# Storing the RWKV states from GpSimd's queue, with the prompt state in another buffer

## The chip, the core and the metric

The kernel runs on one core of one Trainium2 chip. The core has a matrix engine (TensorE, PE in the profile, with its weight loads shown apart as PEld), three engines for elementwise work (VectorE or DVE, ScalarE or ACT, GpSimd or POOL) and a queue engine (SyncE or SP) that does nothing here but issue DMAs. Each engine takes its instructions in a fixed order. The metric is the time of one execution on the device in microseconds; lower is better.

## The reference

One step of a streaming encoder with one layer, for a prompt of 256 tokens and 8 sample sequences of 16 tokens, 384 tokens in all, with a model width of 1024. Cut to what matters here:

```
P = h @ w_in                                  # RWKV part, attention part, two gates
# RWKV-7, 16 heads of 64; for every token, in order:
sa = einsum('bhij,bhj->bhi', S, a)
S  = S * w + sa[..., None] * b + v[..., None] * k
y  = einsum('bhij,bhj->bhi', S, r)
...
m = gate_a * (o_a @ w_proj_a) + gate_b * (o_b @ w_proj_b)
x = x + g1 * (m @ w_out)
x = x + g2 * peer(rmsnorm(x) ...)             # 16,384 experts, top-k
```

The final state `S` of every sequence is an output: `wkv_prompt` (16 heads of 64 x 64) and `wkv_sample` (8 times as much). Nothing else in the program reads these outputs.

## The kernel before, in words

The program has four stages: the input and its modulation; a long stage with RWKV, attention, gates and the rest of the modulation; the mix of both branches; and the experts, which take more than half of the time. The change is in the second stage.

There the method `run` goes through a string `ORDER` and emits one unit of work for each letter: R is a pair of RWKV heads (eight of them, numbered 0 to 7 by `e`), D a quarter of the attention heads, G a gate unit, M a modulation unit. The written program is a list; a planner then makes the order of each engine's queue from it, by simulated time, taking the earlier-written instruction first when several are ready. So on the chip the units overlap, and a later unit fills what an earlier one leaves free. The planner also adds every wait that a buffer or a value needs. When the program changes, all orders are made anew.

Buffers go by tag. In the RWKV pool a tag has one buffer, if not said otherwise, and tiles with one tag take turns in the order in which they are written in the program: a tile can be filled only when all that reads or writes the tile before it, stores included, is done.

One RWKV pair (`rwkv_pair`) goes so:

- Front: three projections `r`, `k`, `v`, elementwise work, and the matrices `MB`, `MK`. The gate's weights are loaded into the tag `gup` (L559, L560) and serve only at the pair's end.
- `rwkv_inverse`: a triangular inverse. Its 16 x 16 blocks are solved row by row on VectorE (L708, L710) between several DMA round trips through DRAM (L693 to L722). Then two levels merge the blocks. Each level begins with a GpSimd multiplication into the tag `NO` (L727), which PE reads at once (`cp<-TN,NO` in the profile), and ends with L742.
- `chain_p`: the prompt's four chunks in sequence. The states `H` are written from L791 on, the last one at L805, and L806 stores it.
- `chain_s`: the eight samples. Their states are loaded (L828) into the tag `S0`, updated (L875), multiplied by a decay on GpSimd (L877) and stored (L878).
- End: normalisation and the gate; L686 stores the pair's output to DRAM, and the mix loads the outputs of all pairs at L1185.

The pairs overlap: the front, the row-by-row solution and the first `NO` of pair e+1 are made while pair e is in its chains. The two levels of pair e+1 use a PSUM tag (`cp`) that both chains use too.

The lines on which the prediction's steps rest:

```python
726:  NO = self.t([128, 4, 64], tag="NO")
727:  nc.gpsimd.tensor_tensor(NO, MB[:, :, 0:64], ..., op=OP.mult)
770:  H = self.t([128, 4, 64], tag="gup")
806:  nc.sync.dma_start(self.O["wkv_p"][:, e], H[:, 3])
877:  nc.gpsimd.tensor_tensor(S0, S0, ..., op=OP.mult)
878:  nc.sync.dma_start(self.O["wkv_s"][:, e], S0)
```

Weights come through SP: `raw` (L248) loads 512 KB at a time into the tag `w`, which has four buffers; ScalarE and VectorE split them (L238, L242) for PE, while the modulation units read them as they are.

Of the kernel before, what the change touches and what calls it, by code (L numbers as in the profile page):

```python
# [19 lines left out]
OP = mybir.AluOpType  # L20
# [163 lines left out]
S0, PH = 30, 4  # L184
# [17 lines left out]
class K:  # L202
# [342 lines left out]
    def rwkv_pair(self, e):  # L545
# [106 lines left out]

        H = lambda t: t.rearrange("p i (h d) -> p i h d", d=64)
        B = lambda s: s.unsqueeze(3).to_broadcast([128, 3, 2, 64])
        sm = self.t([128, 3, 2], tag="gnm")
        nc.vector.tensor_reduce(out=sm, in_=H(y), op=OP.add, axis=AX.X)
        nc.vector.tensor_scalar(sm, sm, 1.0 / 64, None, op0=OP.mult)
        nc.vector.tensor_tensor(H(y), H(y), B(sm), op=OP.subtract)
        sq = self.t([128, 3, 128], tag="sq2")
        nc.scalar.activation(sq, y, AF.Square)  # L660
        vr = self.t([128, 3, 2], tag="gnv")
        nc.vector.tensor_reduce(out=vr, in_=H(sq), op=OP.add, axis=AX.X)
        rs = self.rstd(vr, vr, 1.0 / 64, GN_EPS)
        nc.vector.tensor_tensor(H(y), H(y), B(rs), op=OP.mult)
        lw = self.t([128, 2, 128], tag="lnx")
# [3 lines left out]
        L = lambda q: lw[:, q].unsqueeze(1).to_broadcast([128, 3, 128])  # L669
        nc.gpsimd.tensor_tensor(H(vn), H(vn), B(bon), op=OP.mult)  # L670
        nc.gpsimd.tensor_tensor(vn, vn, L(1), op=OP.add)
# [73 lines left out]
    def chain_p(self, e, AR, M, TT, bn, kn, vn, y, DC):  # L745

        nc = self.nc
        MB, MK = M  # L750
        hs = lambda h: slice(h * 64, h * 64 + 64)
        units = [(i, c, h, slice(64 * c, 64 * c + 64), slice(64 * h, 64 * h + 64)) for i in range(2) for h in range(2) for c in range(2)]
        Sb = self.t([128, 3, 2, 64], tag="Sb")
        nc.gpsimd.memset(Sb, 0.0)

        p = self.ps([128, 2, 2, 128], tag="cp")
        for i in range(2):
            nc.tensor.transpose(p[:, i, :, 0:64], AR[:, 0, 2 * i:2 * i + 2].rearrange("p a b -> p (a b)"), self.ident)
        for i, c, h, rr, hr in units:
            self.mm(p[rr, i, h, 64:128], MK[rr, i, h, 0:64], vn[rr, 1 + i, hs(h)], tp=(64 * c, 64 * c))  # L760
        R = self.t([128, 2, 2, 128], tag="S0")
        nc.scalar.activation(R, p, AF.Copy)

        p = self.ps([128, 2, 2, 128], tag="cp")
        for i, c, h, rr, hr in units:
            self.mm(p[rr, i, h], TT[rr, i * 2 + h], R[rr, i, h], tp=(64 * c, 64 * c))
        Q = self.t([128, 2, 2, 128], tag="cQ")
        nc.vector.tensor_copy(Q, p)

        H = self.t([128, 4, 64], tag="gup")  # L770
        G = self.t([128, 3, 64], tag="NX")
        Y = self.t([128, 3, 64], tag="lnx")
        for c, tag in ((0, "cp"), (1, "cs")):
            p = self.ps([128, 3, 2, 64], tag=tag)
            rr = slice(64 * c, 64 * c + 64)
            for i in range(2):
                hh = [(h, slice(64 * h, 64 * h + 64), (64 * c, 64 * h)) for h in range(2)]
                for h, hr, to in hh:
                    self.mm(p[hr, 0, i], bn[rr, 1 + i, hs(h)], Q[rr, i, h, 64:128], start=True, stop=False, tp=to)
                for h, hr, to in hh:  # L780
                    self.mm(p[hr, 0, i], kn[rr, 1 + i, hs(h)], vn[rr, 1 + i, hs(h)], start=False, stop=True, tp=to)
                if i or c:
                    for h, hr, to in hh:
                        self.mm(p[hr, 1, i], Q[rr, i, h, 0:64], bn[rr, 1 + i, hs(h)], tp=to)
                    for h, hr, to in hh:
                        self.mm(p[hr, 2, i], Q[rr, i, h, 0:64], MB[rr, i, h, 64:128], tp=to)
            un = slice(c, 4, 2)
            i0 = 0 if c else 1
            ug = slice(c + 2 * i0, 4, 2)
            u1 = slice(c + 2 * i0 - 1, 3, 2)  # L790
            nc.vector.tensor_tensor(H[:, un], p[:, 0], DC[:, un].unsqueeze(2).to_broadcast([128, 2, 64]), op=OP.mult)  # L791
            nc.vector.tensor_tensor(G[:, u1], p[:, 1, i0:], self.i64.unsqueeze(1).to_broadcast([128, 2 - i0, 64]), op=OP.add)
            nc.vector.tensor_tensor(Y[:, u1], p[:, 2, i0:], AR[:, 1, ug], op=OP.add)
        for h in range(2):
            hr = slice(64 * h, 64 * h + 64)
            nc.vector.tensor_copy(Sb[hr, 0, h], H[hr, 0])
        for un in range(1, 4):
            p = self.ps([128, 64], tag="cp")
            for h in range(2):
                hr = slice(64 * h, 64 * h + 64)  # L800
                self.mm(p[hr], G[hr, un - 1], Sb[hr, un - 1, h], tp=(64 * h, 64 * h))
            for h in range(2):
                hr = slice(64 * h, 64 * h + 64)
                out = Sb[hr, un, h] if un < 3 else H[hr, 3]
                nc.vector.scalar_tensor_tensor(out, p[hr], DC[hr, un:un + 1], H[hr, un], op0=OP.mult, op1=OP.add)  # L805
        nc.sync.dma_start(self.O["wkv_p"][:, e], H[:, 3])  # L806
        p = self.ps([128, 2, 128], tag="cp")
        cc = [(c, slice(64 * c, 64 * c + 64)) for c in range(2)]
        for i in range(2):
            for c, rr in cc:  # L810
                un = 2 * i + c
                if un:
                    self.mm(p[rr, i], Y[:, un - 1], Sb[:, un - 1].rearrange("p a b -> p (a b)"), start=(un == (2, 1)[c]), stop=False, tp=(0, 64 * c))
        for i in range(2):
            for h in range(2):
                for c, rr in cc:
                    self.mm(p[rr, i, hs(h)], MB[rr, i, h, 64:128], Q[rr, i, h, 64:128], start=False, stop=False,
                            tp=(64 * c, 64 * c))
                for c, rr in cc:
                    self.mm(p[rr, i, hs(h)], MK[rr, i, h, 64:128], vn[rr, 1 + i, hs(h)], start=False, stop=True,  # L820
                            tp=(64 * c, 64 * c))
        self.cpr = nc.scalar.activation(y[:, 1:3], p, AF.Copy)

    def chain_s(self, e, AR, M, TT, bn, kn, vn, y, DC):
        nc = self.nc
        MB, MK = M
        S0 = self.t([128, 8, 64], tag="S0")
# [36 lines left out]
        for g0 in (0, 2):  # L864
            pp = [self.ps([128, 128], tag=tag) for tag in ("cs", "cp")]
            for q, (src, x) in enumerate(zip((bi, ki), ex)):
                for h in range(2):
                    for gp, p in zip((g0, g0 + 1), pp):
                        gr = slice(32 * gp, 32 * gp + 32)
                        m = self.mm(p[64 * h:64 * h + 64], src[gr, hs(h)], x[gr, h].rearrange("p j d -> p (j d)"), start=(q == 0),  # L870
                                    stop=(q == 1), tp=(32 * gp, 64 * h))
                        if gp == g0 and q == 0:
                            self.after(m, self.cpr)
            for gp, p in zip((g0, g0 + 1), pp):
                self.cpr = nc.vector.tensor_tensor(S0[:, 2 * gp:2 * gp + 2], S0[:, 2 * gp:2 * gp + 2],  # L875
                                                   p.rearrange("p (j d) -> p j d", d=64), op=OP.add)
        nc.gpsimd.tensor_tensor(S0, S0, DC.unsqueeze(2).to_broadcast([128, 8, 64]), op=OP.mult)  # L877
        nc.sync.dma_start(self.O["wkv_s"][:, e], S0)  # L878


    def rope(self, dst, x, which, n):
# [914 lines left out]
```

## Time and profile before

| | |
|---|---|
| median of three runs | 1747.88 us (1744.3 to 1750.02) |
| the profiled execution's own time | 1744.26 us |
| its span, first to last instruction | 1742.5 us |
| PE busy | 1666.7 us (96%) |
| VectorE busy | 1353.8 us (78%) |
| ScalarE busy | 745.2 us (43%) |
| GpSimd busy | 544.0 us (31%) |
| DMA, mean | 251 GB/s |

The span is what the profile covers; the execution's own time has 1.8 us more. PE's ends are modelled, so its busy time is not time at its peak; its idle time is what the waits are read from. The state stores are 8 x 256 KB (`out_wkv_s`) and 8 x 32 KB (`out_wkv_p`), the first at 257.2 us, the last at 683.3 us.

### The profile page before, as it was taken

The page shows a single profiled execution, that of the slowest core. Times are in us where ns is not written, and L with a number is a line of the kernel's source. Part 1 is how long each engine was busy: PE and PEld are TensorE (multiplying, and loading weights), DVE is VectorE, ACT ScalarE, POOL GpSimd, SP SyncE. Part 2 cuts the span into 40 slices and gives each one's busy share as a digit, 9 for nine tenths or more (in the row PEclk, how much of TensorE's full clock was granted, in tenths as well). Part 3 has the DMA queues.
Part 4 walks back from the last instruction along what each step waited for, and adds up shares of the span by engine and source line. Part 5 has one row for each costly group of instructions (what it writes and reads, how often), then busy time and mean ns, then how long its engine had stood idle before and what let it go on. Part 6 is the DMA issues. An engine that isn't in the chain of part 4 may idle for free.

```text
span 1742.5 us, 33102 instructions
## 1 busy us (share of the span) xinstructions
PE 1666.7 (96%) x12376; PEld 1407.1 (81%) x12376; DVE 1353.8 (78%) x2905; ACT 745.2 (43%) x1666; POOL 544.0 (31%) x621
## 2 busy tenths in 40 slices
PE   6999999999999988999999999999989999999997
PEld 4998888877888877998887889999966676776675
DVE  3548878776877865566999998999948788777797
ACT  4543433333343333444323355577844343443343
POOL 2434333232333220034033233441233234332331
PEclk8999999899999999999999999999999999999999
DMA  8543653455365365755398999986479999999993
GB/s 300 167 135 104 209 181 85 135 176 165 91 208 158 97 220 193 250 186 193 122 359 318 368 345 383 392 317 236 165 286 351 368 384 372 395 385 382 353 395 109
DMA packets 173049, 437.23 MB, mean 251 GB/s; under 512 B 46036, under 2 KB 86612, under 8 KB 156504
## 3 DMA queue, kind: packets, MB, share of 16 engines
q1 hardware_dynamic: 154456, 300.89, 50.8%
q0 software_dynamic: 18432, 134.23, 19.8%
q8 instruction: 98, 1.61, 0.4%
q14 instruction: 63, 0.52, 0.1%
HBM read 403.75 MB, written 31.30 MB: 250 GB/s over the span
## 4 chain that ended last, share of the span: by engine, by line
PE 42%; DVE 16%; DMA 6%; issue 5%; ACT 3%; POOL 1%; SPq 0%; DVEq 0%; POOLq 0%; ACTq 0%
PE mm L234 11%; PE fx L234 10%; PE dx L234 8%; PE cp L234 6%; PE bx L234 5%; DVE acc L1616 2%; DVE wl L242 2%; DVE raw L1610 2%; DMA raw<-in_puv,pe 2%; ACT wh L238 1%; DMA w<-in_pv 1%; DMA w<-in_puT 1%; POOL raw L1603 1%; DVE psi L1330 1%; DVE ps L1331 1%
## 5 line engine op out<-in xcount | busy, mean ns | idle before, releaser
L242 DVE TENSOR_TENSOR wl<-w,wh 128x1024 fp32r<-128x1024 f32 x231 | 291.1, 1264 | 88.6 <-ACT wh L238 53.3
L238 ACT ACTIVATE wh<-w 128x1024 fp32r<-128x1024 f32 x239 | 250.6, 1050 | 156.0 <-PE mm L234 66.0
L1603 POOL DMA_INDIRECT raw<-in_puv,pe x100 | 136.9, 1369 | 335.5 <-DVE acc L1616 116.5
L234 PE MATMUL fx<-h2h,wl 128*128 128x256 f32 x688 | 194.7, 284 | 5.6 <-DVE wl L242 5.6
L234 PE MATMUL fx<-h2h,wh 128*128 128x256 f32 x688 | 196.2, 285 | 1.6 <-ACT wh L238 1.4
L234 PE MATMUL fx<-h2l,wh 128*128 128x256 f32 x688 | 192.9, 281 | 0.0
L234 PEld LDWEIGHTS fx<-h2h,wl 128*128 128x128 f32 x688 | 129.8, 189 | 8.2 <-DVE wl L242 7.4
L1616 DVE SCALAR_TENSOR_TENSOR acc<-raw,dots,acc 128x1024 f32<-128x1024 f32 x99 | 128.9, 1302 | 8.7 <-ACT dots L1612 8.6
L234 PEld LDWEIGHTS fx<-h2h,wh 128*128 128x128 f32 x688 | 129.6, 188 | 6.5 <-ACT wh L238 3.7
L234 PEld LDWEIGHTS fx<-h2l,wh 128*128 128x128 f32 x688 | 129.7, 189 | 1.6 <-issue 1.2
L1610 DVE SCALAR_TENSOR_TENSOR raw<-raw,sh 128x1024 f32<-128x1024 f32 x100 | 123.8, 1238 | 4.8 <-DMA raw<-in_puv,pe 4.7
L234 PE MATMUL mm<-LTh,wh 128*128 128x384 f32 (+2 forms) x352 | 124.1, 353 | 1.9 <-ACT wh L238 1.1
L234 PE MATMUL mm<-LTh,wl 128*128 128x384 f32 (+2 forms) x352 | 123.5, 351 | 0.4 <-DVE wl L242 0.4
L234 PE MATMUL mm<-LTl,wh 128*128 128x384 f32 (+2 forms) x352 | 122.1, 347 | 1.1 <-POOL LTl L495 1.1
L234 PE MATMUL mm<-h2f,w 128*128 128x256 f32 x464 | 105.4, 381 | 0.0
L1611 ACT ACTIVATE dots<-dots 128x1 f32<-128x1 f32 x128 | 25.5, 199 | 183.8 <-DVE raw L1610 150.8
L234 PE MATMUL mm<-wh,LTh 128*128 128x256 f32 x336 | 99.3, 296 | 1.0 <-ACT qx L898 1.0
L234 PE MATMUL mm<-wh,LTl 128*128 128x256 f32 x336 | 99.2, 295 | 0.0
L234 PE MATMUL mm<-wl,LTh 128*128 128x256 f32 x336 | 98.6, 294 | 0.0
L234 PEld LDWEIGHTS mm<-h2f,w 128*128 128x128 f32 x464 | 87.5, 190 | 12.4
L234 PE MATMUL fx<-h2f,w 128*128 128x256 f32 x336 | 79.4, 390 | 0.0
L234 PEld LDWEIGHTS fx<-h2f,w 128*128 128x128 f32 x336 | 65.2, 196 | 9.9 <-issue 0.5
(609 smaller groups left out, 4435.3 us busy)
## 6 DMA issues: line engine op xcount, KB each, us to landing
w<-in_puT SPq DMA_DIRECT2D x119, 512.0 KB, 6.3
w<-in_pv SPq DMA_DIRECT2D x85, 512.0 KB, 7.3
w<-in_w_in SPq DMA_DIRECT2D x70, 512.0 KB, 4.6
w<-in_w_ada SPq DMA_DIRECT2D x48, 512.0 KB, 4.7
G<-in_pv SPq DMA_DIRECT2D x43, 512.0 KB, 7.1
cKT<-in_cKT SPq DMA_DIRECT2D x32, 256.0 KB, 4.6
cV<-in_cV SPq DMA_DIRECT2D x32, 256.0 KB, 4.1
w<-in_w_pq SPq DMA_DIRECT2D x16, 512.0 KB, 4.4
```

Of the source, the lines that this page charges most:

```text
L234: return self.nc.tensor.matmul(out, l, r, start=start, stop=stop, skip_group_check=True, **kw)
L238: self.nc.scalar.activation(hi, src, AF.Copy)
L242: (self.nc.vector if eng == "v" else self.nc.gpsimd).tensor_tensor(lo, src, hi, op=OP.subtract)
L1330: nc.vector.max_index(si[:, half, h, 0:8], sv[:, half, h, 0:8], s[:, c])
L1331: nc.vector.match_replace(out=s2, in_to_replace=sv[:, half, h, 0:8], in_values=s[:, c], imm_value=MARK)
L1603: d = nc.gpsimd.indirect_dma_start(out=bass.AP(tensor=u.tensor, offset=u.offset, ap=[u.ap[0], [1, 2048]]), out_offset=None, in_=self.I["puv"],
L1610: nc.vector.scalar_tensor_tensor(u, u, 1.0, h2, op0=OP.mult, op1=OP.mult, accum_out=dot)
L1611: nc.scalar.activation(dot, dot, AF.Gelu_apprx_tanh)
L1616: nc.vector.scalar_tensor_tensor(acc, v, dot, acc, op0=OP.mult, op1=OP.add)
```

## The change

`H` moves from the tag `gup` to the tag `NO`. The prompt state's store is taken out of `chain_p`; the tile is kept in `self.wkvp`. Both stores are now issued by GpSimd at the end of `chain_s`, and `issue_after` puts them behind the multiplication L877 in GpSimd's queue: first the sample states, then the prompt state. The bytes stored are the same.

```diff
-        H = self.t([128, 4, 64], tag="gup")
+        H = self.t([128, 4, 64], tag="NO")
...
-        nc.sync.dma_start(self.O["wkv_p"][:, e], H[:, 3])
+        self.wkvp = H
...
-        nc.gpsimd.tensor_tensor(S0, S0, DC.unsqueeze(2).to_broadcast([128, 8, 64]), op=OP.mult)
-        nc.sync.dma_start(self.O["wkv_s"][:, e], S0)
+        m = nc.gpsimd.tensor_tensor(S0, S0, DC.unsqueeze(2).to_broadcast([128, 8, 64]), op=OP.mult)
+        with self.tc.issue_after(m.ins):
+            nc.gpsimd.dma_start(self.O["wkv_s"][:, e], S0)
+            nc.gpsimd.dma_start(self.O["wkv_p"][:, e], self.wkvp[:, 3])
```

## The prediction

> **What bounds the kernel now.** I began with the page, then took the stretch in which the changed lines run, 230 to 697 us, and split it where the last RWKV pair begins.
>
> ```profile
> span 1742.5 us, 33102 instructions
> ```
>
> ```profile
> 230.00:627.00 397.00, 389.75 (x4467) 332.10 (x4465) 309.46 (x828) 141.70 (x353) 136.30 (x216) 0.98 0.47 139
> 627.00:697.00 70.00, 60.85 (x702) 48.43 (x700) 38.22 (x94) 25.48 (x61) 5.59 (x6) 0.98 0.71 241
> ```
>
> After the stretch's length come busy us of PE, PEld, DVE, ACT and POOL, the granted clock, the DMA share and GB/s. PE is busy for 389.75 of 397 us and for 60.85 of 70: its idle time is 7.2 + 9.2 = 16.4 us. POOL has 5.6 us of work in the last 70. So this stage is PE's, and all that a smoother queue could give back here is 16.4 us. Next I asked which waits make up PE's idle time there, and how long SP stands at the lines that the change touches.
>
> ```profile
> PE cp L758 <- DVE TT L742: 3.5, 1, 3.5
> PE mm L234 <- DMA w<-in_w_ada: 3.1, 1, 3.1
> ```
>
> ```profile
> SPq L806 <- DVE gup L805: 19.4, 5, 11.2
> ...
> SPq L878 <- POOL S L877: 13.1, 3, 8.9
> ...
> SPq L559 <- DMA out_wkv_p<-gup: 8.2, 5, 4.6
> ```
>
> SP stands 19.4 us before the prompt state's store, 13.1 us before the sample states' store, and 8.2 us before the next `gup` load, whose buffer that store still reads: 40.7 us in all. But PE's longest waits are a single 3.5 us for a step of the block inverse, and a single 3.1 us for a weight load. SP's 40.7 us hardly reach PE, because loads are made several buffers ahead.
>
> **The change part by part.** *Removed from SP:* 16 issues and the three waits. An issue costs SP about 0.35 us:
>
> ```profile
> L806 SPq DMA_DIRECT2D out_wkv_p<-gup x8: 343/353/382, 257.2 to 670.5; - x8
> ...
> DMA to landing us min/median/max: 1.5/1.7/5.5
> ```
>
> ```profile
> L878 SPq DMA_DIRECT2D out_wkv_s<-S x8: 344/377/1401, 270.5 to 683.3; - x8
> ...
> DMA to landing us min/median/max: 2.1/3.5/8.0
> ```
>
> That is 16 x 0.36 = 5.8 us of SP, beside PE's work: 0. The waits are worth something only where a load behind them is what PE waits for. That happens once, in the 3.1 us for `w_ada`, so I followed that load. The longest stand at L806 (11.2 us) is shortly ahead of it.
>
> ```profile
> 624.43 1.91 PE L234 MATMUL mm<-w,cst 128*32 128x256 f32 x26
> ...
> 627.59 0.68 PE L234 MATMUL cp<-TN,NO 64*64 64x64 f32 x16
> ```
>
> ```profile
> 626.74 0.91 SPq L248 DMA_DIRECT2D w<-in_w_ada  x2
> ```
>
> The matmuls that empty the `w` buffers in use end at 624.43 + 1.91 = 626.34; the loads go out at 626.74. However empty SP had been, they could have gone 0.4 us sooner. I take **-0.4 us**; bounds: 0, and -9.2 us if every idle moment of the last 70 us came from late loads. The `gup` loads come earlier too, but serve only the end of a pair: 0.
>
> *Added to POOL:* 16 DMA issues behind the multiplication L877. No plain DMA is issued by POOL in this trace; the nearest row is its indirect load of 128 rows.
>
> ```profile
> L1603 POOL DMA_INDIRECT raw<-in_puv,pe x100: 935/1146/3490, 871.1 to 1683.3; - x100
> ```
>
> The smallest was 0.94 us, the median 1.15, the largest 3.49. An SP issue of 0.35 is the bound from below. I take 0.95, since a plain store has no list of rows to read: 15 us of POOL over the stage, which has 325 us idle there (467 - 136.3 - 5.6): 0 as work. What is queued behind the two issues on POOL is 1.9 us later, once for each pair: small multiplications and copies of the next pair, on which PE waits nowhere in the long rows above.
>
> *Moved: the prompt state's buffer.* This is the step that I weigh most. `H` now lies in the single buffer `NO`, which the next pair's block inverse fills at L727. The buffer is free only when the `wkv_p` store has landed, and that store now stands behind L877 and the `wkv_s` store. Today L727 is done far ahead, even before `H` of the pair before is written:
>
> ```profile
> 595.40 0.73 POOL L727 TENSOR_TENSOR NO<-MBp,cfront 128x256 f32<-128x256 f32 x1 [4.05 <-DVE MBp L635]
> ...
> 626.60 1.04 POOL L877 TENSOR_TENSOR S<-S,DCs 128x512 f32<-128x512 f32 x1 [1.66 <-DVE S L875]
> 628.37 0.75 POOL L727 TENSOR_TENSOR NO<-MBp,cfront 128x256 f32<-128x256 f32 x1 [0.72 <-PE cp L234]
> ```
>
> ```profile
> 603.01 0.28 DVE L791 TENSOR_TENSOR gup<-cp,DCp 128x128 f32<-128x128 f32 x1
> ```
>
> The last pair's `NO` is written at 595.40, `H` of pair 6 from 603.01 on, and the matmuls that read `NO` start at 627.59, when L877 of pair 6 ends (627.64). The same holds in six of the seven handovers. The next view counts PE's work on `NO` (x16 is one whole step) in the 3 us after each L877 ends; only the sixth window is empty.
>
> ```profile
> 270.40:273.40 3.00, 0.68 (x16) 0.54 (x16) 0.65 (x1) 1.00 0.29 93
> 319.70:322.70 3.00, 0.68 (x16) 0.54 (x16) 0.19 (x1) 1.00 0.57 189
> 380.50:383.90 3.40, 0.68 (x16) 0.54 (x16) 0.00 (x0) 1.00 0.79 266
> 443.60:446.60 3.00, 0.68 (x16) 0.54 (x16) 1.05 (x1) 1.00 0.23 87
> 498.40:501.40 3.00, 0.68 (x16) 0.55 (x16) 0.74 (x1) 1.00 1.01 392
> 556.90:559.90 3.00, 0.00 (x0) 0.00 (x0) 0.00 (x0) 1.00 0.90 246
> 627.50:630.50 3.00, 0.68 (x16) 0.54 (x16) 0.75 (x1) 1.00 0.86 261
> ```
>
> The new wait, counted from the end of L877: two issues of 0.95; then `wkv_p`'s flight, between its own 1.7 - 0.35 = 1.35 and what `wkv_s` ahead of it needs, 0.95 + 3.5 - 0.35 = 4.1 from the end of L877; then 0.75 for L727. So PE can start at +4.0 to +4.9 us. Today it starts between 0 and +3; I take 0.7 as typical, and 3.3 to 4.2, say 3.8 us, as what each of six handovers loses. From below it is 1 us (starts at +3 today, fast landing); from above 0.95 + 0.95 + 7.65 + 0.75 - 0 = 10.3 (the slowest landing, 8.0, counted after both issues).
>
> In five of these handovers I count it at nothing. What covers it is PE's other work: the projection, gate and attention matmuls of later units, which fill PE to 98% up to 627, and which are planned around the wait. What is late next is the pair's own chain, and it is repaid only if other work is still left at the end. So the last handover decides. There the pair comes 4.0 to 4.9 us later, and this is the room at its end:
>
> ```profile
> d<-sq SPq DMA_DIRECT2D x8, 192.0 KB, 1.9
> ```
>
> ```profile
> 686.34 0.32 SPq L686 DMA_DIRECT2D d<-sq  x1
> 692.21 0.80 SPq L1185 DMA_DIRECT2D px<-d  x2
> ```
>
> The last pair's output goes out at 686.34 and lands by 688.2 (median 1.9); the first loads of the mix go at 692.21, held by attention's last matmuls. Room is 4.0 us, so 0 to 0.9 us is left over; I take **+0.9**. The sum is 0 - 0.4 + 0 + 0.9 = **+0.5 us**.
>
> The profiled execution took 1744.26 us (span 1742.5 and 1.8 around it), 3.6 below the median of the runs, so its sum is 1744.8; on the median it is 1747.88 + 0.5, or **1748.4 us**.
>
> [...]
>
> **Rivals.** *Slower: the handover is on PE's path.* PE takes its work in a fixed order. If, in that order, the matmuls on `NO` come before they can start, PE idles for what is left of the wait. It decides as soon as the other work put between L877 and these matmuls is shorter than 4.0 us. For it: six of seven handovers start at once today, and idle time in the last 70 us is already 9.2 us, so other work is short there. Against: the order is made anew with the wait known, and PE is nearly full. Price: with no cover 6 x 3.8 = 23 us; with half of it covered 11 us, or 1759.
>
> *Slower: POOL's issues are stretched.* The slowest indirect issue took 3.49 us instead of 0.94; if each plain one did, the wait would grow by 2 x 2.5 = 5 us at each of six handovers, 30 us without cover and 15 with half, or 1763. Against: the median is 1.15. [...]
>
> *Faster: SP's freedom pays.* If the loads behind L806, L878 and L559 spread out, the idle time of the last 70 us would go (9.2 us), or 1739. For it: 40.7 us of SP's waiting. Against: the one load that PE waited for was held by its buffer.
>
> *The change doesn't do what it says:* the stores leave SP, but SP then stands before what comes next (the loads of a later step), and all orders shift a little. That gives a few us to either side, 1743 to 1753, and a little more if it lands badly.
>
> **How the numbers follow.** Less than 0.3%, 5.2 us, can't be told from no change here. The forecast, with the quiet part of the last rival, has 0.45 and its own range is 1743 to 1753. The handover on PE's path has 0.23, stretched issues 0.04; SP's freedom 0.22; a reshuffled order past the bound 0.03 to either side. That makes 0.25 faster, 0.45 same, 0.30 slower. The range leaves out the full prices at either end: 1737 (just past the 9.2 us) to 1763 (15 us slower).
>
> **What would show it.** Right: no store of either state in SP's rows, POOL issues near 0.95 us, L727 of the next pair idle until `wkv_p` has landed, its matmuls 4 to 5 us after L877, and PE's idle time in this stage still about 16 us. Wrong: PE waits on `NO` of several us at several handovers, or the last 70 us shrink. If PE's idle time is the same and the time still moves by over 5 us, the cause is outside these steps.

## The result and the profile after

The changed kernel takes 1768.9 us (median of seven runs, 1765.1 to 1779.1) against 1747.88 us; the ratio is 1.0143, with a 95% interval of 1.0120 to 1.0167 (the two medians alone give 1.0120). It is slower, and the forecast (1748.4 us, no change) was wrong. The profiled execution is the slowest of the seven, 1779.07 us, so its trace shows some 10 us more than the median. Lines behind L877 are two higher than before; the stores are now L879 and L880.

First the page's head, and PE's busy time by stretch, split as before where the second last pair's L877 ends (627 us then, 652 now). The columns are those of the prediction.

```profile
span 1777.3 us, 33128 instructions
```

```profile
230.00:652.00 422.00, 404.38 (x4507) 341.94 (x4510) 321.73 (x835) 143.59 (x355) 150.48 (x229) 0.96 0.45 134
652.00:729.00 77.00, 65.78 (x683) 52.68 (x679) 37.50 (x91) 25.43 (x59) 9.13 (x11) 0.90 0.61 207
```

PE's idle time in the stage is 17.6 + 11.2 = 28.8 us instead of 16.4, and the granted clock is 0.96 and 0.90 instead of 0.98 and 0.98. Outside the stage little moved: from the mix's first matmul to the end it is 1048.1 us against 1045.9. PE's longest waits of the stage, in the view of waits:

```profile
PE mm L234 <- DMA d<-qr: 5.2, 1, 5.2
PE mm L234 <- ACT wh L238: 4.0, 2, 3.6
PE dx L234 <- DVE set L1110: 2.6, 3, 1.9
PE cp L234 <- DVE TT L742: 1.8, 1, 1.8
...
PE mm L234 <- DMA w<-in_w_ada: 1.4, 1, 1.4
```

None of them names `NO`. The wait is there, but GpSimd has it, and hardly PE. The view of single lines for the store of the prompt state, the store of the sample states, and L727:

```profile
L880 POOL DMA_DIRECT2D out_wkv_p<-NO x8: 578/634/809, 272.6 to 714.5; - x8
...
  POOL NO L727: 5.3, 3
```

```profile
L879 POOL DMA_DIRECT2D out_wkv_s<-S x8: 539/542/602, 273.5 to 716.4; - x8
...
DMA to landing us min/median/max: 2.3/2.4/3.0
```

```profile
L727 POOL TENSOR_TENSOR NO<-MBp,cfront x16: 717/736/2240, 162.6 to 669.7; 128x256 f32<-128x256 f32 x16
...
  DMA out_wkv_p<-NO: 5.3, 3
...
  PEld cp L234: 2.2, 1
```

GpSimd stands idle before L727 for 5.3 us, in three handovers, until the prompt state has landed; on PE's side a single weight load waits 2.2 us for L727. An issue costs GpSimd 0.63 or 0.54 us, and the planner issues the small store first although it is written second. What a handover from one pair to the next looks like now is seen in the timelines of GpSimd and of PE at the fifth (start, duration, engine, line):

```profile
529.63 1.09 POOL L877 TENSOR_TENSOR S<-S,DCs 128x512 f32<-128x512 f32 x1
530.67 0.63 POOL L880 DMA_DIRECT2D out_wkv_p<-NO  x1
531.31 0.54 POOL L879 DMA_DIRECT2D out_wkv_s<-S  x1
...
533.84 0.82 POOL L727 TENSOR_TENSOR NO<-MBp,cfront 128x256 f32<-128x256 f32 x1
```

```profile
530.73 0.34 PE L234 MATMUL mm<-LTl,wh 128*128 128x384 f32 x1
...
536.61 0.27 PE L590 MATMUL fx<-cfirst,sq 128*128 128x128 f32 x1
536.81 0.68 PE L234 MATMUL cp<-TN,NO 64*64 64x64 f32 x16
```

L877 ends at 530.72; `NO` is ready at 534.66, 3.9 us later; PE doesn't stand still, it works on a projection (`mm`), and comes to the `NO` matmuls at 536.81, 6.1 us after L877, where it came 0.1 us after it before.

The next table gives this for all seven handovers: us from the end of L877 to the end of the first `NO` product, and to the first matmul that reads it, both read from the timelines. The last two kernels are experiments told below.

| kernel | NO ready | matmuls on NO start |
|---|---|---|
| before | -41, -37, -48, -50, -42, -3, -32 | 1.5, 2.0, 2.7, 0.8, 0.1, 21.9, -0.1 |
| after | 2.8, 4.5, 4.3, 3.4, 3.9, 3.8, 6.6 | 5.6, 8.8, 7.9, 4.0, 6.1, 3.9, 17.0 |
| the change in the order of before | 2.7, 2.6, 4.6, 3.7, 5.0, 6.5, 6.5 | 2.8, 2.7, 4.7, 3.7, 5.1, 21.8, 6.6 |
| wait and queue taken out, order of after | 1.3, 4.4, 3.3, 1.3, 3.7, 0.9, 2.3 | 5.8, 7.8, 6.8, 4.0, 6.7, 4.1, 14.3 |

The starts add up to 28.9 us before and 53.3 after. The last L877 ends at 714.6 instead of 683.2, 31.4 us later, and the mix begins 32.6 us later; 24.4 us of it are in these starts, if the pairs are taken as one chain.

### The profile page after: what moved, and what is told of

It is laid out like the page before. It is cut to its first block, busy times and chain, and to the rows that moved or that the text cites. A ratio compares the mean times of both kernels' runs of the same rounds, so it can differ in the third digit from the quotient of the medians.

```text
span 1777.3 us, 33128 instructions
## 1 busy us (share of the span) xinstructions
PE 1689.5 (95%) x12376; PEld 1425.7 (80%) x12376; DVE 1362.6 (77%) x2905; ACT 746.9 (42%) x1666; POOL 566.6 (32%) x637
## 4 chain that ended last, share of the span: by engine, by line
PE 59%; DVE 18%; DMA 11%; issue 6%; ACT 3%; POOL 2%; SPq 1%; DVEq 0%; POOLq 0%; ACTq 0%
PE mm L234 20%; PE dx L234 12%; PE fx L234 11%; PE cp L234 8%; PE bx L234 7%; DMA raw<-in_puv,pe 2%; DVE wl L242 2%; DVE acc L1618 2%; DVE raw L1612 2%; DMA w<-in_w_in 1%; DMA w<-in_pv 1%; ACT wh L238 1%; DMA w<-in_puT 1%; DVE TX L708 1%; DMA d<-MBp 1%
## 5 line engine op out<-in xcount | busy, mean ns | idle before, releaser
L234 PEld LDWEIGHTS mm<-LTh,wh 128*128 128x128 f32 (+2 forms) x352 | 67.9, 193 | 11.7 <-ACT wh L238 6.8
```

The costliest lines, as they stand in the source:

```text
L234: return self.nc.tensor.matmul(out, l, r, start=start, stop=stop, skip_group_check=True, **kw)
```

## The experiments

Three theories. *W:* the wait at the handover, `NO` being late, carries the loss. *Q:* the 16 issues on GpSimd's queue carry it. *O:* the planner makes the order anew for every variant, and it is the order that costs. The first four expectations are older than these names: their theory 1 is W, and their rivals are the issues on GpSimd's queue and a re-made order. Ratios are against runs of the kernel before on the same chip in the same session, with 95% intervals.

**The parts one by one.** First the buffer without the queue:

```diff
-        H = self.t([128, 4, 64], tag="gup")
+        H = self.t([128, 4, 64], tag="NO")
```

> Only the buffer: H in the tag NO, both stores on SP as before. Theory 1 (handover: the next pair's first multiplication into NO waits for the prompt store that stands behind L877): here the prompt store goes out at its old place, some 12 us ahead of L877, so NO is free in time, the matmuls on NO start 0 to 3 us after L877 as before, and the time is that of before, 1743 to 1753 us. Rival A (GpSimd's queue: the DMAs that it issues are what costs): also 1743 to 1753. Rival B (any change makes new orders, and these happen to be worse): no reason to be near either, 1735 to 1775.

1753.4 us, ratio 1.0044 (1.0030 to 1.0057). Then the queue without the buffer, once with the prompt state still in `gup`, once with the last prompt state in a 256-byte tile of its own:

```diff
-        nc.sync.dma_start(self.O["wkv_p"][:, e], H[:, 3])
+        self.wkvp = H
...
-        nc.sync.dma_start(self.O["wkv_s"][:, e], S0)
+        with self.tc.issue_after(m.ins):
+            nc.gpsimd.dma_start(self.O["wkv_s"][:, e], S0)
+            nc.gpsimd.dma_start(self.O["wkv_p"][:, e], self.wkvp[:, 3])
```

> Only the queue: both stores on GpSimd behind L877, H in the tag gup as before. Theory 1: nothing that the next pair needs early waits for the store (gup serves only a pair's end), so the matmuls on NO start 0 to 3 us after L877 and the time is 1743 to 1753 us. Rival A: the whole loss, 1764 to 1774 us. Rival B: 1735 to 1775.

1765.8 us, ratio 1.0101 (1.0061 to 1.0141).

```diff
+        L = self.t([128, 64], tag="Hl")
...
-                out = Sb[hr, un, h] if un < 3 else H[hr, 3]
+                out = Sb[hr, un, h] if un < 3 else L[hr]
```

> Both stores on GpSimd behind L877, and the final prompt state alone in a buffer of its own (256 bytes a partition); the rest of H stays in gup. Nothing waits for the store but the next pair's final state. Theory 1: 1740 to 1753 us, the matmuls on NO 0 to 3 us after L877. Rival A: 1764 to 1774 us. Rival B: 1735 to 1775, and not the same as the run with the queue alone.

1759.9 us, ratio 1.0081 (1.0057 to 1.0105). The first lies in rival A's range, the second below it. In neither does `NO` wait for a store, the starts of the `NO` matmuls add up to 34.7 and 30.4 us, close to before, and both are slower all the same. So W alone can't be the whole. The counterpart is the wait alone, on the kernel before:

```diff
-        nc.sync.dma_start(self.O["wkv_s"][:, e], S0)
+        self.held = nc.sync.dma_start(self.O["wkv_s"][:, e], S0)
...
+            first = nc.gpsimd.tensor_tensor(NO, ...)
+            if lev == 0 and self.held is not None:
+                self.after(first, self.held)
```

> The kernel before, stores on SP and H in gup, with one thing added: the next pair's first multiplication into NO waits until the sample states' store has landed, as if it shared a buffer with it. Wait after L877: 3.5 us to land and 0.75 for the multiplication, 4.3 us, where it is 0.7 today. Theory 1: 3.6 us at each of six handovers, 1763 to 1773 us, the matmuls on NO 4 us or more after L877. Rival A: 1743 to 1753. Rival B: 1735 to 1775.

1768.9 us, ratio 1.0132 (1.0092 to 1.0173): the whole loss, with nothing on GpSimd's queue. A smaller dose, where the first `NO` waits only for L877:

```diff
-        nc.gpsimd.tensor_tensor(S0, S0, DC.unsqueeze(2).to_broadcast([128, 8, 64]), op=OP.mult)
+        self.held = nc.gpsimd.tensor_tensor(S0, S0, DC.unsqueeze(2).to_broadcast([128, 8, 64]), op=OP.mult)
```

> The kernel before with one wait added: the first NO product of the next pair waits until the last multiplication of this pair is done, but not for any store. In the variant that also waits for the landing of the large store (1768.9 us, ratio 1.013) NO comes some 3 us later at each of 7 handovers. Theory W, dose by dose: the idle time of PE in the stage lies between that of before (16 us) and of that variant (27 us), and the time at 1754 to 1762 us. Theory O: the order is re-made here too, so the time is that of any re-made order, 1753 to 1768 us, and does not follow the idle time.

1751.1 us, ratio 1.0047 (1.0025 to 1.0068). PE's idle time in the stage was 11.9 us, below that of before, so the dose that W gave for the idle time is not seen, and the time came out 3 us below W's range and 2 below O's, which its interval doesn't separate from either. And in all five kernels the planner had made PE's order anew: in the traces, of PE's 12376 matmuls in order of start, between 2062 and 4445 places hold one of another tile or shape than before. Each of these runs therefore mixes two things.

**Order and change taken apart.** First, what an edit costs that leaves the planned order of PE, ACT and GpSimd as it was: the small tile `Hl` alone, both stores on SP.

> The kernel before with one edit: the final prompt state (the 256 bytes per partition that wkv_p stores) goes into a small tile of its own, Hl, and is stored from it on SP's queue at the old place. The planned order of PE, ACT and POOL is that of the kernel before, instruction for instruction; the tile H comes free one store earlier. It is the measure of what an edit of the source does when the order stays. Theory O (the order that the planner re-makes for each variant carries most of the loss): 1744 to 1748 us, ratio 1.000. Theory Q (GpSimd's stores themselves cost): the same. Theory W (the wait at the handover carries it): the same. If it is off by over 0.3%, differences of 0.4% between variants mean nothing.

1746.0 us, ratio 0.9995 (0.9979 to 1.0012): nothing, with PE's order as before but for 2 places. Then the order was held by hand. At the end of the program each engine's instructions are chained in the order of another kernel, by edges that carry no wait and add no instruction (the kernel before, pinned to another order, has 33102 instructions as without the pinning). No kernel was pinned to its own order, so what the pinning itself costs is not measured; the next run, in which pinning and moved stores cost 0.25% together, bounds it.

```diff
         K(ctx, tc, I, O).run()
+        pin(tc, ('PE', 'DVE', 'Activation', 'Pool', 'SP'))
...
+            for a, b in zip(order, order[1:]):
+                tc.add_manual_dep(ins[b], ins[a].name, dep, reason="pin")
```

The queue variant with its own tile, in the order of the kernel before:

> The kernel with the stores on GpSimd's queue and the prompt state in its own small tile (1759.9 us, ratio 1.008), but with the instructions of all five engines pinned to the order that the kernel before has; only the 16 stores stand elsewhere, behind the last multiplication of each pair. No wait is added or taken away by the pinning. Theory O: 1744 to 1749 us, ratio 0.999 to 1.002: the 0.8% of the variant was the order. Theory Q: 1756 to 1762 us, ratio 1.007 to 1.010, since the stores are still GpSimd's. Theory W: there is no handover wait here, so 1744 to 1749; it leaves the 0.8% of the unpinned variant without a cause.

1749.7 us, ratio 1.0025 (1.0010 to 1.0040), down from 1.0081: just above O's range and far below Q's. The reverse, the kernel before in the order of the queue variant, and the small-tile kernel in that of its queue variant, both with all stores on SP:

> The kernel before, unchanged (prompt state in gup, both stores on SP), but with the instructions of all five engines pinned to the order that the planner made for the variant with the stores on GpSimd's queue and the old buffer (1765.8 us, ratio 1.010). Its store never makes the next pair wait, and GpSimd issues nothing. Theory O (an order that is merely another one costs): 1757 to 1764 us, ratio 1.007 to 1.011, so that GpSimd's own issues are worth 0.3% at most. Theory Q (the issues on GpSimd's queue cost): 1743 to 1748 us, ratio 0.999 to 1.002.

1753.6 us, ratio 1.0055 (1.0033 to 1.0077), below O's range and above Q's.

> The same for the variant with the stores on GpSimd's queue and the prompt state in its own small tile (1759.9 us, ratio 1.008): stores on SP at the old places, all five engines pinned to that variant's order. With the order of before, that variant had 1.0025. Theory O: 1753 to 1757 us, ratio 1.004 to 1.007. Theory Q: 1743 to 1748 us.

1754.4 us, ratio 1.0046 (1.0028 to 1.0064), as O gave. Order and queue add up: 0.46% + 0.25% is 0.7% where 0.8% was measured together. So another order costs about 0.5% here even where no part of the change is in the kernel, and the stores as GpSimd issues them cost 0.25 to 0.5%. Issued there they are also late: the prompt state's goes out when L877 ends, some 13 to 17 us later than before. To tell the issuing engine from the lateness, both stores were written behind L877, but on SP's queue:

```diff
-        nc.sync.dma_start(self.O["wkv_p"][:, e], H[:, 3])
+        self.wkvp = L
...
         nc.sync.dma_start(self.O["wkv_s"][:, e], S0)
+        nc.sync.dma_start(self.O["wkv_p"][:, e], self.wkvp)
```

> The kernel before with the prompt state in its own small tile, and both stores on SP's queue behind the last multiplication of the pair: the stores are as late as in the changed kernel, but SP issues them. The planned order of PE, ACT and POOL is that of the kernel before. Theory Q, small form (the 0.25% that is left with the order of before held is the price of 16 issues on GpSimd): 1744 to 1747 us, ratio 0.998 to 1.001. If it is the lateness of the prompt store instead: 1748 to 1751 us, ratio 1.002 to 1.004.

1746.8 us, ratio 1.0005 (0.9992 to 1.0017). But the edit doesn't do what its expectation says. The prompt store is written late and issued early, because the planner puts it where its tile is ready:

```profile
L880 SPq DMA_DIRECT2D out_wkv_p<-Hl x8: 343/353/2087, 255.3 to 670.1; - x8
```

L877 ends between 268.6 us (first pair) and 682.5 us (last) in this run, so each prompt store goes out 12 to 17 us ahead of it, as before. The run repeats the small tile alone and says nothing of lateness. Whether the 0.25% comes from GpSimd's issues, from the late prompt store or from the pinning is not shown. Little speaks for the lateness: in the pinned queue variant the views of both stores name nobody who waited for them.

**The wait and the order of the changed kernel.** Now the order that the changed kernel has, on a kernel that has its buffer, but both stores on SP, so that neither the wait for the store nor the queue is left (GpSimd's order still has the `NO` product behind L877):

> The kernel with the prompt state in an NO buffer and both stores on SP's queue (1753.4 us, ratio 1.004), but with the instructions of all five engines pinned to the order that the changed kernel has; the prompt store lands early, so nothing of the next pair waits for the end of this one. The stores are not GpSimd's. Theory O: 1763 to 1770 us, ratio 1.010 to 1.014, nearly all of the loss of the changed kernel without its wait and without its queue. Theory W: 1750 to 1757 us, ratio 1.003 to 1.007: with the wait gone PE fills its handovers again. Theory Q: 1753 us, as the buffer alone.

1765.7 us, ratio 1.0119 (1.0097 to 1.0141), in O's range. By these ratios five sixths of the loss are in the order alone, the place of the `NO` product behind L877 included. The view of what waited for L727 there, and the rows of the last handover:

```profile
L727 POOL TENSOR_TENSOR NO<-MBp,cfront x16: 721/735/2227, 161.0 to 658.1; 128x256 f32<-128x256 f32 x16
...
  PEld cp L234: 2.1, 1
  PEld fx L234: 0.2, 1
```

```profile
644.50 0.73 POOL L727 TENSOR_TENSOR NO<-MBp,cfront 128x256 f32<-128x256 f32 x1
```

```profile
657.30 0.68 PE L234 MATMUL cp<-TN,NO 64*64 64x64 f32 x16
```

The rows behind the first are who waited for it: weight loads of PE, 2.1 + 0.2 us in all. `NO` is ready at 645.23, and PE comes to it at 657.30, because its order puts other matmuls first, with which it is busy for 10.7 of these 12.1 us. The lateness is written into the order.

Last, the change itself in the order of before. All instructions are pinned but the 16 stores and the 16 `NO` products, which have to go behind L877:

> The changed kernel itself, with the instructions of all five engines pinned to the order that the kernel before has. Left free are only the 16 stores and the 16 NO products, which stood ahead of the last multiplication on GpSimd and have to stand behind it now. So the next pair's NO waits for the landing of wkv_p, as in the changed kernel, but TensorE's order makes no room for that wait. Theory O (it is the re-made order that costs, the wait as such does not): 1748 to 1754 us, ratio 1.002 to 1.005, and the idle time of PE in the stage stays at 15 to 20 us. Theory W (the wait costs, and the re-made order is the planner's way to pay it): NO comes some 5.5 us behind the last multiplication, while the matmuls of before started 1.5, 2.0, 2.7, 0.8, 0.1, 21.9 and -0.1 us behind it; that is 4.0 + 3.5 + 2.8 + 4.7 + 5.4 + 0 + 5.6 = 26 us of new idle time of PE, so 1765 to 1780 us, ratio 1.012 to 1.020, and the idle time of the stage at 35 to 45 us.

1763.1 us, ratio 1.0105 (1.0087 to 1.0123), just below W's range and far above O's. Here PE does stop, and its waits say where:

```profile
PE cp L234 <- POOL NO L727: 17.1, 6, 6.6
PE dx L1108 <- ACT se L1100: 2.7, 3, 1.3
```

One such handover in the timelines of GpSimd and of PE:

```profile
501.91 0.67 POOL L880 DMA_DIRECT2D out_wkv_p<-NO  x1
502.58 0.54 POOL L879 DMA_DIRECT2D out_wkv_s<-S  x1
505.62 1.38 POOL L727 TENSOR_TENSOR NO<-MBp,cfront 128x256 f32<-128x256 f32 x1 [2.50 <-DMA out_wkv_p<-NO]
```

```profile
502.87 0.33 PE L234 MATMUL bx<-XG,guh 96*128 96x384 f32 x1
507.05 1.12 PE L234 MATMUL cp<-TN,NO 64*64 64x64 f32 x16 [3.85 <-POOL NO L727]
```

Two issues, 2.50 us until `wkv_p` has landed, the product, and PE is idle for 3.85 us. The six stops sum to 17.1 us where W had worked out 26; other idle time shrank, so that the stage has 26.2 us in all, between O's 15 to 20 and W's 35 to 45, where the pinned queue variant has 17.8. Against the pinned queue variant, which has the same order and the same queue but no wait, the step is 1.05% - 0.25% = 0.8%, some 14 us, known to about 4 us to either side: the price of the wait in the old order.

What follows: the wait costs some 14 us where the order makes no room for it. The planner does make room, and PE then has no long stop at `NO`; but the order with that room costs 1.2% by itself, no less than the stops with their 0.8%. Either way the last pair ends later and so does the stage. The stores on GpSimd's queue add 0.25%, and 1.2 + 0.25 is the measured 1.4%, though each of the three numbers is known only to about 0.2%. Of the 1.2%, about 0.5% is what other orders cost that have no late `NO`; that the rest is the deferred handover is argued from the table and not shown. What in the moved stores costs the 0.25 to 0.5% was not found. No variant beats the kernel before.

## Why the prediction was wrong, step by step

- *"In five of these handovers I count it at nothing. What covers it is PE's other work."* This step failed. The other work is there, as the fifth handover shows, but it isn't free: the order that puts it into the handovers costs 1.2% by itself, some 21 us, where the prediction has nothing; and with the old order kept, the same wait costs 0.8%. Why the new order costs is shown in part only: that work taken forward is missing later, and that the pair behind comes later for it, is read off the table of handovers. The prediction said so itself, "repaid only if other work is still left at the end", and then priced the last handover alone. At the end of the stage the attention quarter's output is now what the mix waits for, where the longest such wait of a mix matmul was 1.5 us before (`pbh` from ScalarE):

```profile
723.58 0.44 PE L1121 MATMUL dx<-cfirst,ob 128*128 128x128 f32 x2 [0.52 <-DVE ob L1118]
729.20 1.01 PE L234 MATMUL mm<-pbh,wh 128*128 128x384 f32 x2 [5.18 <-DMA d<-qr]
```

- The wait's size was right: `NO` was forecast at 4.0 to 4.9 us after L877 and came at 2.8 to 6.6, 4.2 on average. The working was not: issues of 0.63 and 0.54 us instead of 0.95, and the small store first, not behind the large one. That the size came out right is in part luck.
- *The last handover, +0.9:* the room of 4.0 us was taken from the old order. In the changed kernel the last `NO` came at 6.6, its matmuls at 17.0, and between the issue of the last output's store (722.4) and the mix's first load (724.4) there were 2.0 us, where there were 5.9 before. The load waits 1.2 of them for that store to land: nothing of the room was left.
- *SP's freedom, -0.4:* the wait for `w_ada` fell from 3.1 to 1.4 us in the trace after, but SP's freedom bought no time: in the order of before, the kernel whose SP issues none of these stores still waits 3.1 us for `w_ada`, and it is 0.25% slower, not faster. That rival fell.
- *GpSimd's 16 issues, 0:* the stores on its queue cost 0.25%, some 4 us, in the old order; that the issues themselves do it is not shown. *Stretched issues:* no issue of these stores took over 0.81 us in the trace after; this rival fell.
- *The handover on PE's path* was right in its place, with 0.23. Its full price of 23 us needs no cover; held in the old order it is some 14 us, with 17.1 us of stops. Its argument against, "the order is made anew with the wait known", was the trap: the new order costs no less.
- *Reshuffled orders* had "a few us to either side". The planner made six other orders in these runs, and all six kernels are slower, by 0.4 to 1.4%; two of these orders, borrowed without the moved stores, cost 0.5% each, and the changed kernel's own 1.2%. Nothing lay on the other side.
- What would show it: the sign "no store of either state in SP's rows" came true. The matmuls, forecast at 4 to 5 us after L877, came 3.9 to 17.0 after it, only two of seven near 4, and PE's idle time, forecast at about 16 us, was 29: by its own test the forecast was wrong. But PE's "waits on `NO` of several us", the sign for the rival, didn't come either.

## What to carry to other kernels

Where a planner makes the order, an edit is priced twice: once with the order held, and once for the order that it sets off. Pin the instructions of one version in the order of the other, both ways, before blaming a queue or a buffer, and read in the trace where an instruction was issued before you trust where it is written. And in a stage like this one, whose bound engine is 97% busy and which runs along a chain of units, don't put a wait that is "covered by other work" at nothing: here the order that covered it cost 1.2%.

## What the runs showed of the hardware that was not expected

At the ends of two long stops PE's granted clock was 0.50. In the pinned run of the change, these are the stretches behind two of the new stops (the clock is the third number from the end of a row; the others as above):

```profile
500.00:503.20 3.20, 3.20 (x27) 1.82 (x15) 3.20 (x11) 2.06 (x5) 2.19 (x3) 1.00 0.57 159
506.00:512.80 6.80, 5.75 (x61) 3.72 (x61) 1.96 (x5) 3.51 (x7) 2.05 (x4) 0.50 0.44 134
...
630.00:638.00 8.00, 7.92 (x105) 5.12 (x103) 6.09 (x15) 4.57 (x14) 3.80 (x4) 1.00 0.53 122
642.70:649.40 6.70, 4.73 (x69) 3.83 (x71) 1.17 (x3) 1.33 (x2) 1.45 (x2) 0.50 0.80 307
```

The same order without the wait, in the pinned queue variant, has 1.00 in the stretch of the first stop, and 0.76 in the one behind the last handover:

```profile
502.00:509.00 7.00, 7.00 (x66) 6.06 (x64) 4.12 (x8) 3.45 (x8) 1.11 (x2) 1.00 0.99 346
...
632.00:639.00 7.00, 6.04 (x59) 3.93 (x60) 2.40 (x4) 3.56 (x8) 0.00 (x0) 0.76 1.04 409
```

The stop of 3.85 us ends at 507.05, the one of 6.58 us at 644.7, and each is followed, from before its end on, by 6.7 or 6.8 us at 0.50. The stops of 0.63 to 2.75 us in that run were followed by none. In other traces the length of a gap doesn't decide whether half clock follows. In the kernel before, a gap of 3.14 us that ends at 634.66 was followed by 1.00 up to 687 us. In the trace after, a gap of 1.81 us that ends at 609.18 was followed by 6.8 us at 0.50. In the kernel before, a stretch of 10.2 us at 0.50, in which PE was busy throughout, came behind gaps of 0.34 and 0.98 us:

```profile
302.12 0.33 PE L234 MATMUL cp<-Sb,NX 64*64 64x64 f32 x4 [0.34 <-DVE Sb L805]
303.43 0.66 PE L234 MATMUL bx<-W,TTs 128*128 128x64 f32 x4 [0.98 <-DVE W L845]
```

```profile
305.20:315.40 10.20, 10.20 (x70) 8.93 (x65) 7.96 (x18) 2.34 (x6) 3.78 (x4) 0.50 0.24 77
```

What sets the clock is not shown.

For the changed kernel, gaps and clock nearly close the sum. The stage reaches from the first `NO` matmul to the first matmul of the mix; the idle time is the sum of PE's gaps; half of the time at half clock is taken as lost, an estimate from the granted 0.50 (in the trace after, the 128x256 matmuls of a projection start every 0.21 us at 0.50, from 612.74 to 615.72, and every 0.12 us at 1.00, from 603.72 to 604.67):

| kernel | stage | PE idle | at half clock | stage - idle - half of that |
|---|---|---|---|---|
| before | 481.1 | 16.4 | 17.1 | 456.1 |
| after | 512.2 | 29.3 | 47.8 | 459.0 |
| the change in the order of before | 496.9 | 26.2 | 35.9 | 452.8 |
| queue variant in the order of before | 483.7 | 17.8 | 20.5 | 455.7 |
| wait and queue out, order of after | 500.1 | 23.7 | 35.8 | 458.5 |
| small tile alone | 487.0 | 14.7 | 35.5 | 454.6 |
| before in the order of the queue variant | 487.8 | 16.5 | 19.3 | 461.6 |

The last column has nearly the same matmuls in each (5308 to 5318 of them), but not the same time: by this estimate 28 of the 31 us between before and after are gaps and clock, and about 3 are not. Over all fourteen traces it is 452.8 to 456.1 us in the five kernels with the old order, and 457.0 to 462.2 us in the nine with another. So in a new order PE was also busy longer with the same matmuls, beyond what the clock accounts for by this estimate. In the last row this is nearly all of the loss: 6.7 us of stage, 5.5 of them in the last column, with gaps and clock almost as before. Why was not found. One profile alone is no measure of the clock: the small tile's run has as much half-clock time as the change in the order of before (35.5 and 35.9 us), at a time equal to the kernel before. Over all runs the time given away, estimated as span x (1 - granted clock), is 29.9 us before (mean of 15 runs) and 40.9 us after (of 7): by this, 11 of the 24 us between these two sets are the clock's. For the last row's kernel it is 31.0 us (12 runs), against 30.7 in the 22 runs of before beside it: 0.3 us more given away in its order.
